# A decoder layer on one core: projection columns reordered, differential heads made two jobs, output projection begun at the sparse heads' rows, late modulation moved to VectorE

## The chip, the cores and the metric

The kernel runs on one core of one Trainium2 chip. The metric is the device time of one execution in microseconds (us). The engines are TensorE (PE in the profile; PEld is its loading of weights into the array), VectorE (DVE), ScalarE (ACT), GpSimd (POOL) and SyncE (SP), which here issues nearly all the transfers from HBM. Each engine works through its own queue in order; an instruction that waits holds up everything behind it on that engine.

## The reference

One layer of a transformer on 256 tokens of width 2048, all in float32, batch 1:

```python
mod = silu(c) @ w_ada + b_ada                          # 2048 x 12288, six chunks of 2048
shift_a, scale_a, gate_a, shift_f, scale_f, gate_f = split(mod, 6)
h = rms_norm(x, g_attn_pre) * (1 + scale_a) + shift_a
d_q, d_k, d_v, s_q, s_k, s_v, i_q, i_k, i_w = split(h @ w_in)      # 2048 x 5456
# partial rotary on d_q, d_k, s_q, s_k, i_q, i_k
diff_out = (softmax(q1 k1) - lam * softmax(q2 k2)) @ d_v           # 8 heads, causal
diff_out = rms_norm(diff_out, g_diff_sub) * (1 - lam_init)
score = sum over 16 heads of i_w * relu(i_q i_k)                   # the indexer
dsa_out = softmax(s_q s_k over the 64 best keys by score) @ s_v    # 8 heads, causal
mixed = concat(diff_out, dsa_out) @ w_o                            # 2048 x 2048
x = x + gate_a * rms_norm(mixed, g_attn_post)
h = rms_norm(x, g_ffn_pre) * (1 + scale_f) + shift_f
ff = (silu(h @ w_gate) * (h @ w_up)) @ w_down                      # d_ff = 5632
out = x + gate_f * rms_norm(ff, g_ffn_post)
```

## The kernel before, in words

**Weight products.** The 256 tokens are two tiles of 128 (t = 0, 1); the rows of a weight matrix are K tiles of 128. `wload` (line 148) brings a block of weights, one megabyte as a rule (4 K tiles x 512 columns), into one of RAW = 5 buffers `raw`, and splits it exactly into two parts: ScalarE copies the high part `whi` (line 168), VectorE subtracts it to get the low part `wlo` (line 169), each over 1024 columns at a time, into WB = 3 buffers each. `mm3` (line 176) makes three products for every K tile and token tile: high by high, high by low, low by high (lines 178, 181, 182).

**Modulation.** `ada_block` (line 191) queues the products of silu(c) with columns of w_ada in units of one megabyte. A unit is either made on TensorE (line 225; the K tiles go to four column groups of the array side by side) or on VectorE (line 233: acc = w * c + acc, 512 columns at a time). One call of `ada_step` uses one unit, and loads run AHEAD = 2 units ahead. `ada_cols` makes shift and scale as columns, for `modA` (attention) and `modF` (feed-forward), `ada_gate` makes the gates `Ga` and `Gf` as rows. Of each gate and of `modF` there are four blocks of 512 columns. On VectorE are two blocks of `Ga` (GA_DVE), one of `modF` (F_DVE) and all of `Gf`; the rest is on TensorE. A block's sums are turned to columns by small products at lines 282 (made on TensorE) or 286 (made on VectorE).

**Input projection.** The rows are taken in five groups of 1, 1, 2, 4 and 8 K tiles (GROUPS), each over all 5456 columns, since the modulation of a group must be known before its products; partial sums are collected in `PR` (line 733). The last group goes column block by column block, 512 wide (the last, number 10, is 336 wide), in the order (0, 2, 4, 10, 9, 8, 1, 3, 5, 6, 7); each column block is two megabyte blocks. 0 to 5 are the queries, keys and values of the differential heads, 6 and 7 the queries of the sparse heads, 8 to 10 the shared key and value, the indexer and its weights. After each column block `attend` rotates the columns and puts jobs in a list: `diff_head` (five stages s0 to s4, one job for each of 8 heads), `idx_pairs`, `top_k`, `dsa_pair` (four stages, one job for each pair of sparse heads). `attn_step` moves every job in flight by one stage and admits the next one of the list; it is called once after each megabyte block. `ada_step` is called there too, with RATE (1, 1, 1, 2) units.

**Output projection.** Row block a = 0, 4, 8, 12 of w_o (rows 0 to 7 of its 16 K tiles are the differential heads', 8 to 15 the sparse heads'), for column blocks 0 and 1 together; before each, `need_mix` runs stages until the heads of these rows are written to `mixT`. Column blocks 2 and 3 follow in `tail_pair`, which ends token tile 0 before token tile 1, so that the norm (`residual`, line 836) and the transposed, modulated input `H2` of the feed-forward (`h2_tiles`, line 826) begin early. After each block there is one `ada_step` and one `attn_step`.

**Feed-forward.** The second half of `H2` (K tiles 8 to 15) needs the second half of `modF`. So the first NSPLIT = 2 column blocks of w_gate and w_up are first multiplied over K tiles 0 to 7 alone (line 875, the half phase), the sums parked in `part` (line 887) and completed later (line 909); meanwhile up to FRATE = 2 modulation units follow each block.

**Order of instructions.** The program text gives the dependences and the priority; the order on each engine is laid out by a planner with estimated times, which takes the earliest instruction in the text that is ready. Only instructions marked `keep_in_program_order` keep their place.

## Time and profile before

| | us |
|---|---|
| median of 3 runs | 1275.33 |
| lowest and highest run | 1273.48, 1276.99 |
| profiled execution: span from first to last instruction | 1272.5 |
| TensorE busy | 1233.9 |
| VectorE busy | 774.3 |
| ScalarE busy | 560.9 |
| GpSimd busy | 21.4 |

The profiled execution's time is recorded as its span alone. A busy time counts an instruction from its start to its end; the ends of matmuls are modelled and products overlap their successors, so the distance between the starts of two products says more about TensorE than their durations. A float32 product (modulation, transposes, attention) appears as two instructions; weight products appear as one each. The stages stand at: input projection's last group until about 395 us, output projection 395 to 511.5, feed-forward from about 516.

### The profile page before, as it was taken

How to read it: one execution, taken by the hardware profiler on the slowest of the kernel's cores; microseconds unless marked ns; L12 is line 12 of the kernel's file. 1: busy time of each engine (PE TensorE's matmuls, PEld its weight loads, DVE VectorE, ACT ScalarE, POOL GpSimd, SP SyncE). 2: the span in 40 equal slices, each digit the busy share in tenths (PEclk: the TensorE clock that was granted, in tenths of full speed). 3: DMA queues.
4: the chain of work that ended last, by engine and by line, in shares of the span. 5: the costliest groups of instructions: out<-in, count | busy, mean ns of one | idle time of the engine just before them, and what ended most of it. 6: DMA issues, size and time to landing. Idle time of an engine off the chain costs nothing.

```text
span 1272.5 us, 15272 instructions
## 1 busy us (share of the span) xinstructions
PE 1233.9 (97%) x5938; PEld 950.3 (75%) x5938; DVE 774.3 (61%) x1160; ACT 560.9 (44%) x806; POOL 21.4 (2%) x55
## 2 busy tenths in 40 slices
PE   4999999999999999899999999999999999999996
PEld 3666666777666786688887888888888888888885
DVE  3576455898598683758867545754455454445565
ACT  4733333345345543764444444444444334444442
POOL 1000000000000000200000000000000000000000
PEclk8999999999999999999999999999999999999998
DMA  9999997978687487858878656766556555565541
GB/s 307 339 343 327 347 381 278 314 263 321 211 285 268 142 329 289 306 167 286 282 264 290 200 193 222 251 227 198 176 189 199 190 188 190 194 198 182 184 164 66
DMA packets 160090, 310.13 MB, mean 244 GB/s; under 512 B 5785, under 2 KB 19978, under 8 KB 158738
## 3 DMA queue, kind: packets, MB, share of 16 engines
q1 hardware_dynamic: 159938, 309.14, 70.7%
q8 instruction: 46, 0.75, 0.2%
q14 instruction: 26, 0.21, 0.0%
q10 hardware_dynamic: 80, 0.02, 0.0%
HBM read 307.05 MB, written 2.10 MB: 243 GB/s over the span
## 4 chain that ended last, share of the span: by engine, by line
PE 88%; DMA 4%; DVE 4%; issue 1%; ACT 1%; SPq 1%; POOL 0%; DVEq 0%; POOLq 0%; ACTq 0%
PE mm L181 26%; PE mm L178 26%; PE mm L182 25%; PE ad L225 5%; DMA raw<-in_w_ada_dram 4%; DVE aacc L233 2%; DVE wlo L169 1%; PE tr L474 1%; PE tr L411 1%; PE tr L918 1%; PE tr L830 1%; SPq L211 1%; PE tr L392 1%; PE tr L301 0%; PE tr L282 0%
## 5 line engine op out<-in xcount | busy, mean ns | idle before, releaser
L169 DVE TENSOR_TENSOR wlo<-raw,whi 128x1024 fp32r<-128x1024 f32 (+1 forms) x383 | 462.3, 1212 | 338.6 <-ACT whi L168 337.7
L168 ACT ACTIVATE whi<-raw 128x1024 fp32r<-128x1024 f32 (+1 forms) x383 | 400.3, 1050 | 522.4 <-PE mm L182 458.1
L181 PE MATMUL mm<-wlo,h 128*128 128x512 f32 (+1 forms) x1056 | 416.8, 395 | 1.9 <-DVE wlo L169 1.9
L182 PE MATMUL mm<-whi,h 128*128 128x512 f32 (+1 forms) x1056 | 409.9, 389 | 0.2 <-DVE h L335 0.2
L178 PE MATMUL mm<-whi,h 128*128 128x512 f32 (+1 forms) x1056 | 381.4, 394 | 2.4 <-ACT h L330 1.4
L181 PEld LDWEIGHTS mm<-wlo,h 128*128 128x128 f32 x1056 | 198.9, 188 | 62.5 <-issue 9.5
L178 PEld LDWEIGHTS mm<-whi,h 128*128 128x128 f32 x1056 | 196.8, 188 | 63.2 <-issue 13.6
L182 PEld LDWEIGHTS mm<-whi,h 128*128 128x128 f32 x1056 | 198.3, 188 | 42.5 <-issue 3.0
L181 PE MATMUL mm<-wlo,gT 128*128 128x512 f32 x348 | 135.8, 390 | 0.0
L182 PE MATMUL mm<-whi,gT 128*128 128x512 f32 x348 | 135.4, 389 | 0.0
L178 PE MATMUL mm<-whi,gT 128*128 128x512 f32 x348 | 123.0, 390 | 0.0
L233 DVE SCALAR_TENSOR_TENSOR aacc<-raw,csil,aacc 128x512 f32<-128x512 f32 x126 | 94.1, 746 | 23.8 <-DMA raw<-in_w_ada_dram 22.5
L225 PE MATMUL ad<-raw,c 128*32 128x512 f32 (+2 forms) x640 | 79.6, 537 | 9.9 <-DMA raw<-in_w_ada_dram 9.9
L733 DVE TENSOR_TENSOR PR<-mm,PR 128x512 f32<-128x512 f32 (+1 forms) x88 | 57.1, 669 | 41.2 <-PE mm L182 41.0
L182 PEld LDWEIGHTS mm<-whi,gT 128*128 128x128 f32 x348 | 65.3, 188 | 13.8 <-issue 0.2
L181 PEld LDWEIGHTS mm<-wlo,gT 128*128 128x128 f32 x348 | 65.3, 188 | 13.7 <-issue 0.2
L178 PEld LDWEIGHTS mm<-whi,gT 128*128 128x128 f32 x348 | 65.3, 188 | 13.4
L181 PE MATMUL mm<-wlo,mixT 128*128 128x512 f32 x124 | 49.1, 397 | 0.0
L178 PE MATMUL mm<-whi,mixT 128*128 128x512 f32 x124 | 47.5, 400 | 0.6 <-ACT mixT L587 0.6
L182 PE MATMUL mm<-whi,mixT 128*128 128x512 f32 x124 | 46.4, 399 | 0.0
L225 PEld LDWEIGHTS ad<-raw,c 128*32 128x32 f32 x640 | 17.6, 116 | 36.4 <-issue 31.3
L181 PEld LDWEIGHTS mm<-wlo,mixT 128*128 128x128 f32 x124 | 23.3, 188 | 7.8 <-issue 2.5
(195 smaller groups left out, 678.8 us busy)
## 6 DMA issues: line engine op xcount, KB each, us to landing
raw<-in_w_ada_dram SPq DMA_DIRECT2D x96, 1024.0 KB, 7.1
raw<-in_w_gate_dram SPq DMA_DIRECT2D x44, 1024.0 KB, 5.2
raw<-in_w_up_dram SPq DMA_DIRECT2D x44, 1024.0 KB, 5.1
raw<-in_w_down_dram SPq DMA_DIRECT2D x44, 1024.0 KB, 5.2
raw<-in_w_in_dram SPq DMA_DIRECT2D x39, 1024.0 KB, 6.9
raw<-in_w_o_dram SPq DMA_DIRECT2D x16, 1024.0 KB, 5.0
xx<-in_x_dram SPq DMA_DIRECT2D x2, 1024.0 KB
x<-in_x_dram SPq DMA_DIRECT2D x2, 1024.0 KB, 4.7
```

The source lines that it names most:

```text
L168: ACT.activation(hv, src, AF.Copy)
L169: DVE.tensor_tensor(lv, src, hv.bitcast(F32), op=ALU.subtract)
L178: i = PE.matmul(ps, lhsT=hi, rhs=whi, start=start, stop=False)
L181: PE.matmul(ps, lhsT=hi, rhs=wlo, start=False, stop=False)
L182: PE.matmul(ps, lhsT=lo, rhs=whi, start=False, stop=stop)
L211: SP.dma_start(st[b, u], ada_w[u * kk * P:(u + 1) * kk * P, col0s[b]:col0s[b] + n] .rearrange("(k p) n -> p k n", p=P))
L225: PE.matmul(st["ps"][32 * j:32 * j + 32, :n], lhsT=c33[:, k, 1 - b:33 - b], rhs=w, start=(b == 0 and k < 4), stop=(b == nb - 1 and k >= 12 ...
L233: DVE.scalar_tensor_tensor(acc, w, csil[:, k:k + 1], acc, op0=ALU.mult, op1=ALU.add)
L392: PE.transpose(tr[:, i * P:(i + 1) * P], PR[:, t, c0:c0 + P], ident)
L411: PE.matmul(sc[i][:, SEG[t]], lhsT=st["q"][r, (2 * j + t) * P:(2 * j + t + 1) * P], rhs=ikT[r, :P * (t + 1)], start=True, stop=True)
L474: PE.matmul(sc[i][:, SEG[t]], lhsT=l, rhs=r, start=False, stop=(t == T - 1))
L733: DVE.tensor_tensor(dst, banks[c0][t][:, :n], dst, op=ALU.add)
```

## The change

- The last group's column order becomes (10, 9, 8, 0, 2, 4, 6, 7, 1, 3, 5).
- `diff_head` makes two jobs: queries and keys to the probabilities (s0 to s2), put in the list after the key columns, and values to `mixT` (s3, s4), put there after the value columns. The probabilities wait in a buffer for five heads. A job has a set of conditions, and `attn_step` admits the first job of the list whose conditions are met; `top_k` waits for all indexer heads, `dsa_pair` for the selection.
- In the last group `attn_step` is called inside the block, after every second K tile: twice per megabyte block, where it was once.
- The output projection takes its first two column blocks in row order 8, 12, 0, 4.
- The second 1024 columns of `modF` are made on VectorE as one block of 1024 columns (before: 512 of them on VectorE, 512 on TensorE). The VectorE halves of `Ga` and all of `Gf` are blocks of 1024 columns too, so an accumulation is 1024 wide.
- RATE becomes (1,), FRATE 1, NSPLIT 4: the half phase covers four column blocks instead of two.
- Buffers are shared: the selection mask takes the indexer keys' place, the rotation's two scratch tiles take that of the heads' outputs, the last split of `tail_pair` that of the second parking buffer. The tile `c33` is made a little later in the text.

The diff, cut to its core:

```diff
-GA_DVE = (2, 3)
-F_DVE = (2,)
-RATE = (1, 1, 1, 2)
-ATT = 1
-FRATE = 2
+RATE = (1,)
+FRATE = 1
-NSPLIT = 2
+NSPLIT = 4
...
-                    hi = more.tile([P, 1024], F32R, tag="xhi", name=nm("xhi"))
-                    lo = more.tile([P, 1024], F32R, tag="xlo", name=nm("xlo"))
+                    both = more.tile([P, 2, 1024], F32R, tag="part", name=nm("xhl"))
+                    hi, lo = both[:, 0], both[:, 1]
...
-            st["acc", b] = wp.tile([P, 512], F32, tag="aacc", name=nm("aacc"), bufs=2)
+            st["acc", b] = wp.tile([P, 1024], F32, tag="aacc", name=nm("aacc"), bufs=2)
...
-    def ada_gate(G, chunk, col, on_pe):
+    def ada_gate(G, chunk, col, n, on_pe=False):
...
-            ps = tr_bank()
-            PE.matmul(ps, lhsT=ones, rhs=accs[0], start=True, stop=True)
-            DVE.tensor_tensor(G[:, col:col + 512], ps, G[:, col:col + 512], op=ALU.mult)
+            for a in range(0, n, 512):
+                ps = tr_bank()
+                PE.matmul(ps, lhsT=ones, rhs=accs[0][:, a:a + 512], start=True, stop=True)
+                g = G[:, col + a:col + a + 512]
+                DVE.tensor_tensor(g, ps, g, op=ALU.mult)
...
-        m1 = pp.tile([P, P], F32, tag="rp1", name=nm("rp1"), bufs=1)
-        m2 = pp.tile([P, P], F32, tag="rp2", name=nm("rp2"), bufs=1)
+        m = pp.tile([P, 2, P], F32, tag="on", name=nm("rp"), bufs=2)
+        m1, m2 = m[:, 0], m[:, 1]
...
-    def attn_step(admit=1):
-        for _ in range(admit):
-            if jobs:
-                active.append(jobs.pop(0))
+    def attn_step():
+        ready = next((j for j in jobs if done.issuperset(j[0])), None)
+        if ready is not None:
+            jobs.remove(ready)
+            active.append(list(ready[1]))
...
-        return [head] + [lambda r=r: rounds(r) for r in range(0, TOPK // 8, 2)] + [tail]
+        return {("idx", i) for i in range(8)}, [head] + [lambda r=r: rounds(r) for r in range(0, TOPK // 8, 2)] + [tail]
...
-            st["a"] = p_T(s[:, 0])
+            p_T(s[:, 0], heads["a"][:, h % 5])
+            done.add(("a", h))
...
-        return [s0, s1, s2, s3, s4]
+        free = {("v", h - 5)} if h >= 5 else set()
+        return (free, [s0, s1, s2]), ({("a", h)}, [s3, s4])
...
-            newjobs.extend([diff_head(4 * (ci - 2) + j) for j in range(4)])
+            for j in range(4):
+                h = 4 * (ci - 2) + j
+                qk, heads[h] = diff_head(h)
+                newjobs.append(qk)
+        elif ci in (4, 5):
+            newjobs.extend([heads[4 * (ci - 4) + j] for j in range(4)])
...
-    order = (0, 2, 4, 10, 9, 8, 1, 3, 5, 6, 7)
+    order = (10, 9, 8, 0, 2, 4, 6, 7, 1, 3, 5)
...
-    for b in range(4):
-        ada_gate(Ga, 2, b * 512, b not in GA_DVE)
+    ada_gate(Ga, 2, 0, 512, True)
+    ada_gate(Ga, 2, 512, 512, True)
+    ada_gate(Ga, 2, 1024, 1024)
     need_ga = len(units)
-    for b in range(4):
-        ada_cols(modF, 3, bF, gF, b * 512, 512, b not in F_DVE)
-        if b == 1:
-            need_f1 = len(units)
+    for b in range(2):
+        ada_cols(modF, 3, bF, gF, b * 512, 512, True)
+    need_f1 = len(units)
+    ada_cols(modF, 3, bF, gF, 1024, 1024, False)
     need_f2 = len(units)
...
+                    if last and k % 2 == 0:
+                        attn_step()
...
                 ada_step(RATE[bi % len(RATE)])
-                for _ in range(ATT):
-                    attn_step()
...
-    for a in (0, 4, 8, 12):
+    for a in (8, 12, 0, 4):
...
-                    mm3(banks[ci, t], mt, k, t, whi, wlo, k == 0, k == KT - 1)
+                    mm3(banks[ci, t], mt, k, t, whi, wlo, k == 8, k == 7)
...
-            for b in range(4):
-                ada_gate(Gf, 5, b * 512, False)
+            for b in range(2):
+                ada_gate(Gf, 5, b * 1024, 1024)
```

## Rows read from the trace of the kernel before

**Rows 1.** The page's first part: busy us, share of the span and instructions of each engine.

```profile
PE 1233.9 (97%) x5938; PEld 950.3 (75%) x5938; DVE 774.3 (61%) x1160; ACT 560.9 (44%) x806; POOL 21.4 (2%) x55
```

**Rows 2.** The order of time on TensorE in the feed-forward: start us, modelled duration us, engine, line, operation.

```profile
799.78 0.39 PE L178 MATMUL mm<-whi,h 128*128 128x512 f32 x1
800.01 0.39 PE L181 MATMUL mm<-wlo,h 128*128 128x512 f32 x1
800.24 0.39 PE L182 MATMUL mm<-whi,h 128*128 128x512 f32 x1
```

**Rows 3.** The table by stretches: stretch in us, its length, then busy us (and instructions) of PE, PEld, DVE, ACT, POOL, granted TensorE clock, DMA share, GB/s.

```profile
235.00:300.00 65.00, 65.00 (x339) 48.51 (x333) 59.80 (x144) 30.84 (x71) 3.54 (x4) 1.00 0.87 305
300.00:395.00 95.00, 95.00 (x502) 61.90 (x502) 68.28 (x189) 41.63 (x82) 1.38 (x2) 1.00 0.74 259
395.00:426.00 31.00, 26.00 (x147) 19.59 (x144) 25.64 (x66) 15.80 (x53) 3.17 (x3) 1.00 0.68 238
...
511.50:523.00 11.50, 7.80 (x56) 3.77 (x56) 8.50 (x15) 7.11 (x17) 5.41 (x9) 1.00 0.82 294
523.00:600.00 77.00, 77.00 (x371) 63.67 (x370) 53.75 (x89) 47.48 (x80) 1.21 (x3) 1.00 0.71 246
...
800.00:840.00 40.00, 40.00 (x178) 33.14 (x177) 23.36 (x24) 17.01 (x17) 0.00 (x0) 1.00 0.84 289
```

**Rows 4.** The chain that ended last, in order of time, around the end of the output projection: start us, us, what (line and number of instructions).

```profile
494.47 0.34 PE tr L286 x4
494.81 0.97 PE ad L225 x2
496.21 0.98 PE ad L225 x2
498.77 1.00 PE ad L225 x8
501.13 0.98 PE ad L225 x4
502.54 0.98 PE ad L225 x2
...
527.64 1.00 PE ad L225 x8
532.95 0.79 PE tr L282 x8
```

**Rows 5.** The order of time on TensorE at the norm between output projection and feed-forward; in brackets the idle time before an instruction and what ended it.

```profile
511.64 2.78 PE L225 MATMUL ad<-raw,c 128*32 128x512 f32 x24
516.57 2.05 PE L830 MATMUL tr<-dg,x 128*128 128x128 f32 x16 [2.15 <-POOL dg L848]
...
519.03 1.06 PE L225 MATMUL ad<-raw,c 128*32 128x512 f32 x8
```

**Rows 6.** The same view at the start of the output projection, three of its waits.

```profile
411.01 0.44 PE L586 MATMUL tr<-ident,on 128*128 128x128 f32 x2 [0.69 <-ACT qT L395]
412.01 0.50 PE L178 MATMUL mm<-whi,mixT 128*128 128x512 f32 x1 [0.56 <-ACT mixT L587]
...
416.87 1.07 PE L495 MATMUL tr<-ident,s 128*128 128x128 f32 x6 [1.13 <-DVE s L519]
```

**Rows 7.** Groups of instructions by line and shape, whole span: line, engine, operation, count, busy us, mean ns of one, idle time of the engine before them and what ended it.

```profile
L169 DVE TENSOR_TENSOR wlo<-raw,whi 128x1024 fp32r<-128x1024 f32 x374 | 455.4, 1223 | 334.9 <-ACT whi L168 334.0
...
L233 DVE SCALAR_TENSOR_TENSOR aacc<-raw,csil,aacc 128x512 f32<-128x512 f32 x126 | 94.1, 746 | 23.8 <-DMA raw<-in_w_ada_dram 22.5
...
L843 DVE SCALAR_TENSOR_TENSOR x<-y,ry,x 128x1024 f32<-128x1024 f32 x4 | 5.0, 1281 | 1.8 <-POOL ry L145 1.8
```

**Rows 8.** The table by stretches again, for DMA (last two columns: share of the 16 engines, GB/s): one row of the whole table, and one of the table for line 233 alone (busy us and count of that line, clock, DMA share, GB/s).

```profile
40.00:80.00 40.00, 38.40 (x207) 26.01 (x210) 32.27 (x54) 22.68 (x37) 0.00 (x0) 1.00 1.00 353
...
460.00:470.00 10.00, 3.85 (x6) 1.00 1.04 385
```

**Rows 9.** Groups by line and shape on VectorE from 235 to 396 us, columns as in rows 7.

```profile
L169 DVE TENSOR_TENSOR wlo<-raw,whi 128x1024 fp32r<-128x1024 f32 x35 | 42.5, 1219 | 13.8 <-ACT whi L168 13.6
L233 DVE SCALAR_TENSOR_TENSOR aacc<-raw,csil,aacc 128x512 f32<-128x512 f32 x29 | 21.6, 744 | 0.1
L733 DVE TENSOR_TENSOR PR<-mm,PR 128x512 f32<-128x512 f32 x16 | 10.7, 682 | 0.1
```

**Rows 10.** The same on TensorE from 235 to 396 us.

```profile
L181 PE MATMUL mm<-wlo,h 128*128 128x512 f32 x120 | 48.9, 407 | 0.0
...
L225 PE MATMUL ad<-raw,c 128*32 128x512 f32 x134 | 18.3, 602 | 0.0
...
L181 PE MATMUL mm<-wlo,mixT 128*128 128x512 f32 x16 | 6.3, 397 | 0.0
...
L182 PE MATMUL mm<-whi,h 128*128 128x336 f32 x16 | 5.1, 318 | 0.0
```

**Rows 11.** The table by stretches (columns as in rows 3) behind the last product and early in the span; the clock is the third column from the end.

```profile
1262.20:1265.60 3.40, 0.00 (x0) 0.00 (x0) 2.55 (x5) 0.72 (x2) 0.00 (x0) 1.00 0.69 255
1265.60:1272.50 6.90, 0.00 (x0) 0.00 (x0) 2.91 (x6) 0.00 (x0) 0.55 (x1) 0.50 0.40 152
...
23.20:33.30 10.10, 7.58 (x69) 4.96 (x69) 0.75 (x3) 1.50 (x4) 0.00 (x0) 0.50 1.10 351
```

More of the change, by code (lines that the diff above doesn't have):

```diff
@@ L206, in load @@
                 if not on_pe:
-                    POOL.memset(st["acc", b], 0.0)
-                SP.dma_start(st["acc", b][0:1], brow)
+                    POOL.memset(st["acc", b][:, :n], 0.0)
+                SP.dma_start(st["acc", b][0:1, :n], brow)
             raw = wp.tile([P, 2048], F32, tag="raw", name=nm("raw"), bufs=RAW)
@@ L293, in ada_cols @@
         ada_block([chunk * D + col, (chunk + 1) * D + col], n, on_pe, finish)
-    def ada_gate(G, chunk, col, on_pe):
+    def ada_gate(G, chunk, col, n, on_pe=False):
         c0 = chunk * D + col
         def finish(accs):
-            ps = tr_bank()
-            PE.matmul(ps, lhsT=ones, rhs=accs[0], start=True, stop=True)
-            DVE.tensor_tensor(G[:, col:col + 512], ps, G[:, col:col + 512], op=ALU.mult)
-        ada_block([c0], 512, on_pe, finish, b_ada[0:1, c0:c0 + 512])
+            for a in range(0, n, 512):
[3 more added lines that the diff above has]
+                DVE.tensor_tensor(g, ps, g, op=ALU.mult)
+        ada_block([c0], n, on_pe, finish, b_ada[0:1, c0:c0 + n])
+    ph1 = ExitStack()
+    pp = ph1.enter_context(tc.tile_pool(name="pp", bufs=1))
+    c33 = ct([P, KT, 33], "c33")
+    POOL.memset(c33, 0.0)
+    DVE.tensor_copy(c33[:, :, 1], csil)
     ssx = ct([P, T], "ssx")
@@ L369, in layer @@
     score = pp.tile([P, 384], F32, tag="score", name="score")
-    nsel = pp.tile([P, 384], F32, tag="nsel", name="nsel")
-    nselb = pp.tile([P, 384], BF16, tag="nselb", name="nselb")
+    nselb = []
     iwS = pp.tile([P, T, 16], F32, tag="iwS", name="iwS")
@@ L424, in pair @@
                 acc_started[0] = True
-        return [s0, lambda: pair(0), lambda: pair(1)]
+            done.add(("idx", p0 + j))
+        return set(), [s0, lambda: pair(0), lambda: pair(1)]
     jobs, newjobs, active = [], [], []
-    def attn_step(admit=1):
-        for _ in range(admit):
-            if jobs:
-                active.append(jobs.pop(0))
+    done = set()
+    def attn_step():
[3 more added lines that the diff above has]
+            active.append(list(ready[1]))
         for j in list(active):
@@ L441, in top_k @@
         m8 = pp.tile([P, T, 8], F32, tag="m8", name="m8")
+        nsel = pp.tile([P, 384], F32, tag="nsel", name="nsel")
         def head():
@@ L458, in tail @@
             DVE.tensor_tensor(nsel, nsel, score, op=ALU.is_equal)
-            DVE.tensor_scalar(nselb, nsel, NEG, None, op0=ALU.mult)
-        return [head] + [lambda r=r: rounds(r) for r in range(0, TOPK // 8, 2)] + [tail]
+            nselb.append(pp.tile([P, 384], BF16, tag="ikT", name="nselb"))
+            DVE.tensor_scalar(nselb[0], nsel, NEG, None, op0=ALU.mult)
+            done.add("sel")
+        return {("idx", i) for i in range(8)}, [head] + [lambda r=r: rounds(r) for r in range(0, TOPK // 8, 2)] + [tail]
     mixT = [None]
@@ L489, in softmax_parts, with p_T @@
         return s, l
-    def p_T(s2d):
+    def p_T(s2d, o=None):
         tr = tr_bank()
@@ L495, in p_T @@
             PE.transpose(tr[:, i * P:(i + 1) * P], s2d[:, i * P:(i + 1) * P], ident)
-        o = pp.tile([P, 384], F32, tag="pT", name=nm("pT"), bufs=2)
+        if o is None:
+            o = pp.tile([P, 384], F32, tag="pT", name=nm("pT"), bufs=2)
         ACT.activation(o, tr[:, :384], AF.Copy)
@@ L536, in s3 @@
             mixed.update((k, k + 1))
-        return [s0, s1, s2, s3]
+        return {"sel"}, [s0, s1, s2, s3]
+    heads = {}
     def diff_head(h):
@@ L543, in diff_head @@
         st = {}
+        if not heads:
+            heads["a"] = pp.tile([P, 5, 384], F32, tag="h1", name="aT")
         def s0():
@@ L555, in s2 @@
             s, l = st["s"], st["l"]
-            rl = st["rl"] = pp.tile([P, 2, T], F32, tag="rcp", name=nm("rcp"), bufs=4)
+            rl = st["rl"] = pp.tile([P, 2, T], F32, tag="rcp", name=nm("rcp"), bufs=6)
             DVE.reciprocal(rl, l)
@@ L562, in s2 @@
                                          s[:, 0, SEG[t]], op0=ALU.mult, op1=ALU.add)
-            st["a"] = p_T(s[:, 0])
+            p_T(s[:, 0], heads["a"][:, h % 5])
+            done.add(("a", h))
         def s3():
-            aT, rl = st["a"], st["rl"]
+            done.add(("v", h))
+            aT, rl = heads["a"][:, h % 5], st["rl"]
             v0, v1 = PR[:, 0, cv:cv + P], PR[:, 1, cv:cv + P]
@@ L790, in side @@
         ada_step(1)
-        for _ in range(ATT):
-            attn_step()
+        attn_step()
     def need_mix(ks):
```

7 lines of the change are left out of this document (1 added, 6 removed).

## The prediction

> **What bounds the kernel now.** Read the page's busy table first: TensorE is busy 97% of the span, VectorE 61% [rows 1]. Busy is not peak, so look next at a stretch of the feed-forward: successive weight products start 0.227 us apart [rows 2], and TensorE has no idle time there [rows 3]. A block (one megabyte of weights: 4 K tiles, 2 token tiles, 3 products) is 24 x 0.2275 = 5.46 us of TensorE. So time is won only by taking instructions off TensorE's queue or by closing its idle time. The table by stages shows where idle time is left: 5.0 us at 395 to 426 (start of the output projection) and 3.7 us at 511.5 to 523 (the norm between output projection and feed-forward, "the seam" below); 235 to 395 has none [rows 3]. The change can reach these two places and the modulation products; I find no edit that reaches the first 235 us (the same instructions in the same order) or the feed-forward behind its half phase.
>
> The profiled span is 1272.5 us, the median of the runs 1275.3; the profiled execution's own time is not recorded, so I put the 2.8 us between them around the span and add the sum to 1275.3.
>
> **The change part by part.**
>
> *1. The last quarter of the feed-forward modulation leaves TensorE.* It is 2 x 16 products of 512 columns; each is two instructions, four products run side by side, and eight instructions take 1.0 us. The records show 58 of its 64 instructions. In the chain of waits six pieces from 494.8 to 527.6 carry them: 0.97 + 0.98 + 1.00 + 0.98 + 0.98 + 1.00 = 5.91 us [rows 4]. The other 24 at 511.64 and 8 at 519.03 stand where TensorE waits for the norm anyway (the next item, the transposes at 516.57, still waited 2.15 us) [rows 5]: taking those away is worth nothing. Bringing the sums to columns changes too: a VectorE block needs 16 one-column products per 1024 columns, so 32 instructions where 16 and 8 stood: 16 more at 0.34 / 4 = 0.085 us are 1.4 us, less the 0.79 us piece at 532.95 [rows 4], +0.6. Together **-5.3 us**, bounds -4.5 and -6.5 (each run of these products also delays the next weight product by some 0.1 us).
>
> *2. Output projection from the sparse heads' rows on.* In the old order the sparse heads come last: when the projection's columns end, two differential heads and all four sparse pairs are unfinished, and TensorE has only rows 0 to 3 of the output weights to work on. Its queue then stands behind attention: 0.69 us for a copied transpose, 0.56 for mixT, 1.13 for the softmax rows [rows 6], 5.0 us in all [rows 3]. In the new order, counting stages as written, all four sparse pairs end a column and a half before the projection does, and four blocks on rows 8 to 15 and two on rows 0 to 3, 6 x 5.46 = 32.8 us, are ready while the last stages of heads 4 to 7 run in the first five of them. I take the whole idle time: **-5.0 us**. Bounds: 0, if the same chains stand in the queue a column earlier, and -6.4 (about nine waits each also lose the 0.16 us by which a product overlaps the next).
>
> *3. Seam.* Chain: VectorE's gating, two additions to the residual of 1.28 us each [rows 7], squares on ScalarE, GpSimd, transposes. The new VectorE modulation may stand before one of its steps: one 1024-wide accumulation, 1.28 us by the nearest row of that form and width [rows 7]. Bounds 0 and two of them, 2.6; I take half of one, **+0.6**.
>
> *4. VectorE and DMA in the longer half phase.* 1024-wide accumulations: 128 x 0.746 = 95.5 us of VectorE become 80 x 1.281 = 102.5 [rows 7]; 7 us more over 1.2 ms on an engine with a third free. What matters is density. Written steps: 22 in the last group and 14 in the output projection leave 12 of the 48 megabytes needed for the second half of h2; the half phase has 16 blocks and does one after each. Such a block costs VectorE 2 x 1.223 + 2 x 1.281 = 5.0 of 5.46 us, and 2.1 MB of DMA in 5.46 us is 384 GB/s. The trace shows 385 GB/s over one stretch of 10 us and 353 over another of 40 us [rows 8]. At 353 the 12 blocks (25.2 MB) need 71.3 us against 65.5: +5.8. Five raw buffers and three split ones run ahead, and four blocks without modulation follow: **+1.0**, bounds 0 and 5.8. The second half of h2 must then be ready when the half phase ends, 4 x 5.46 = 21.8 us later; it hides there. The eight more parked banks cost one copy and one addition each, 0.68 us by the addition of a bank [rows 9], on ScalarE and VectorE, which are busy 47 and 54 of 77 us at 523 to 600 [rows 3].
>
> *5. Denser attention in the projection.* Stages now advance twice per block. Columns 2, 4, 6, 7 (8 blocks) hold on VectorE 16 splits (19.5 us), 8 x 2 accumulations (20.5), 8 additions of a bank (5.5) and top-k with most of the heads. Attention and rotation on VectorE in the whole stage is what is left of 59.8 + 68.3 us after 42.5, 21.6 and 10.7: 53 us, some 50 without narrower forms [rows 3, 9]; a half to two thirds, 25 to 33, falls here: 70 to 79 us. TensorE there has 43.7 us of weights and, by the same shares of its own rest (160 - 3 x 136 x 0.2275 - 48 x 0.155 - 17 = 43 us, by the counts in [rows 10], 17 us being 134 modulation instructions at eight per 1.0; 0.155 us is about 0.2275 scaled to the 336-wide column), 21 to 29 us: 65 to 73. VectorE lags by about 6, up to 14 us where the shares differ; three split buffers are 3 x 2.73 = 8.2 us ahead. In 235 to 300 VectorE was busy 92% and TensorE never idle [rows 3]. So **+1.0**, bounds 0 and 14.
>
> The remaining edits (shared buffers, a prepared constant made later in the text, removed comments) cost nothing: the buffers are handed on only after their readers, which lie earlier in the same queues. If a rotation did wait for a head's buffer, the same lag as in 5 would grow.
>
> Sum: -5.3 - 5.0 + 0.6 + 1.0 + 1.0 = -7.7; 1275.3 - 7.7 = **1267.6 us**.
>
> **Rivals.**
>
> *A. VectorE sets the pace in columns 2 to 7* (the slower side). Top-k is a chain on VectorE alone, so it fills that engine without leaving gaps for the splits, and every weight product waits for its split. Price: the whole lag of 14 instead of 1: 1267.6 + 13 = 1281. It decides from a loss of about 11.5 us, where the gains are spent and 0.3% more. For it: VectorE is denser here than anywhere in the old trace. Against: 235 to 300, where denser work met no idle TensorE [rows 3].
>
> *B. The seam lets the clock fall.* Without the 24 products TensorE idles from 511.6 to 516.6, 4.9 us in one piece. At the end of the span the granted clock was still 1.00 for the 3.4 us after the last product and 0.50 from then on; early on it stood at 0.50 for 10.1 us after sparse work [rows 11]. Half of 10.1 is 5.0: up to 1273. The Trainium skill, TensorE: Matmul & The Clock Gate, section What's actually happening, says the throttled level is the default and activity releases it; by that this edit takes away what kept the clock up, which no row of the seam can show yet.
>
> *C. DMA limits the half phase*: +5.8 instead of +1.0, 1272.4. The Trainium skill, DMA: Bandwidth & Descriptors, section Specifications, gives about 358 GB/s per core from HBM and speaks against this part: an estimate by it is 25.2 / 358 = 70.4 us, +4.9. The trace's 40 us stretch (353) agrees, its 10 us stretch (385) does not.
>
> *D. The reorder does not do what it says*: the waits of part 2 reappear in front of the last column. Only part 1 pays: 1272.6.
>
> *E. Better*: part 2 at -6.4, no costs of 3 to 5: 1263.6, and 1262 with part 1 at its bound.
>
> **How the numbers follow.** Chances: forecast 0.47 (own range 1264 to 1271.4), A 0.18, B 0.09, C 0.07, D 0.06, E 0.13. A run of this kernel can be told from no change at about 0.3%, 3.8 us: faster is below 1271.5, slower above 1279.2. Faster: 0.47 + 0.13 = 0.60. Same: B, C, D, 0.22. Slower: A, 0.18. The range goes from E's better bound to just past A's price: 1261 to 1282.
>
> **What would show it.** Part 1: 64 fewer modulation instructions on TensorE (576), none between 494 and 530. Part 2: idle TensorE at the start of the output projection under 1.5 us. Part 3: the seam's idle time rises to about 5 us on the first wait, at clock 1.00 (0.50 is B). Part 4: the half phase, now twice as long, without idle TensorE; idle with splits waiting for raw is C. Part 5: the last group without idle; weight products waiting for VectorE's splits is A. I am wrong if idle time appears in the projection, or if the stages' TensorE sums fall by less than 5 us.

## The result and the profile after

The changed kernel takes 1290.8 us (median of 4 runs, 1287.8 to 1292.6) where the kernel before took 1274.4 beside it: ratio 1.0123, 95% interval 1.0103 to 1.0143. It is slower by 16.4 us; the forecast was faster by 7.7, and the measured time lies above the whole forecast range, 1261 to 1282. The profiled span is 1287.2 us (before 1272.5). One run of one variant below (new order, values first), 1907.7 us at a mean granted clock of 0.64, is slow and left out of its numbers.

The busy table of the page, changed kernel [rows 1]: TensorE has 64 modulation instructions fewer (line 219, 576 in all) and yet a longer span.

```profile
PE 1228.2 (95%) x5882; PEld 956.8 (74%) x5882; DVE 788.4 (61%) x1118; ACT 564.9 (44%) x813; POOL 20.2 (2%) x52
```

The table by stretches, changed kernel, columns as in [rows 3]:

```profile
235.00:300.00 65.00, 65.00 (x312) 46.66 (x311) 61.56 (x117) 27.02 (x42) 0.95 (x1) 1.00 0.81 294
300.00:350.00 50.00, 50.00 (x260) 36.43 (x259) 36.25 (x93) 23.68 (x50) 0.70 (x1) 1.00 0.77 268
350.00:400.00 50.00, 41.26 (x240) 26.28 (x239) 28.20 (x90) 20.28 (x57) 2.11 (x3) 0.93 0.65 222
400.00:430.00 30.00, 27.74 (x158) 20.70 (x157) 13.63 (x34) 14.23 (x37) 0.00 (x0) 1.00 0.54 192
430.00:480.00 50.00, 40.15 (x173) 30.27 (x172) 30.87 (x63) 20.37 (x59) 3.65 (x4) 0.80 0.50 175
...
500.00:540.00 40.00, 30.86 (x136) 25.34 (x135) 32.37 (x44) 20.62 (x41) 6.36 (x10) 0.87 0.74 262
540.00:620.00 80.00, 80.00 (x379) 66.77 (x378) 52.24 (x62) 41.39 (x59) 1.85 (x2) 1.00 0.73 250
```

Subtract the second number of a row from the first. In the projection, 235 to 350, TensorE has no idle time, although VectorE is busy 61.56 of the first 65 us. Behind it TensorE idles 8.7, 2.3, 9.9 and 9.1 us in the stretches that begin at 350, 400, 430 and 500, together 30.0. The same four stretches before had 0, 5.0, 0.0 and 3.7, together 8.7. The 21.3 us of new idle time, less the 4.5 to 6.5 us by which the modulation was to shorten the same stretch, are 15 to 17, and the spans differ by 14.7: the loss is idle TensorE between 350 and 540 us. The granted clock fell with it: in the kernel before it was 1.00 from 235 to 540, here it was 0.50 (1.2 instead of 2.4 GHz) in four stretches of 350 to 480, 27.3 us together, the longest behind the wait at 441.5:

```profile
441.90:455.60 13.70, 11.45 (x44) 8.75 (x43) 6.62 (x21) 4.57 (x19) 1.38 (x2) 0.50 0.01 1
```

What ends the idle time, from TensorE's order of time in the changed kernel (brackets: idle time before, and what ended it):

```profile
351.25 2.78 PE L219 MATMUL ad<-raw,c 128*32 128x512 f32 x24
...
359.46 1.48 PE L219 MATMUL ad<-raw,c 128*32 128x512 f32 x8 [3.39 <-DMA raw<-in_w_ada_dram]
...
365.61 0.33 PE L601 MATMUL tr<-ident,on 128*128 128x128 f32 x1 [2.77 <-DVE on L595]
...
374.52 0.76 PE L502 MATMUL tr<-ident,s 128*128 128x128 f32 x4 [2.24 <-DVE s L527]
...
404.86 1.06 PE L219 MATMUL ad<-raw,c 128*32 128x512 f32 x8 [2.17 <-DMA raw<-in_w_ada_dram]
...
441.52 0.30 PE L502 MATMUL tr<-ident,s 128*128 128x128 f32 x1 [3.31 <-DVE s L574]
...
463.14 0.50 PE L172 MATMUL mm<-whi,mixT 128*128 128x512 f32 x1 [1.46 <-ACT mixT L602]
...
520.06 0.39 PE L176 MATMUL mm<-xhl,mixT 128*128 128x512 f32 x1
...
527.04 3.76 PE L851 MATMUL tr<-dg,x 128*128 128x128 f32 x16 [6.59 <-POOL dg L869]
...
534.32 0.80 PE L172 MATMUL mm<-whi,h 128*128 128x512 f32 x1 [2.01 <-DMA raw<-in_w_gate_dram]
```

Three kinds of waits make up the 30.0 us. About 15 are the waits of [rows 6], more of them: steps of one head's or pair's chain between TensorE, VectorE and ScalarE, with no weight product to put between. The two waits at L219, 3.39 and 2.17 us, are for weights of the modulation: TensorE had taken three units in a row at 351.25, and the load that it then waited for was issued only at 352.38, when a buffer came free.

```profile
352.38 0.37 SPq L205 DMA_DIRECT2D raw<-in_w_ada_dram  x1
```

The last 9.1 us are the seam's, 2.01 of them for the first weights of `w_gate`. When the values reach `mixT` is told by the instructions on VectorE that write it (count, ns of one, first and last start): heads 0 to 3, then the four sparse pairs.

```profile
L603 DVE SCALAR_TENSOR_TENSOR mixT<-tr,g,mixT x4: 477/478/481, 351.0 to 367.7; 128x256 fp32r<-128x256 f32 x4
L542 DVE TENSOR_TENSOR mixT<-tr,mixT x4: 683/684/684, 380.2 to 414.6; 128x512 fp32r<-128x512 f32 x4
```

The projection's last product starts at 350.9 us (before 375.5, not the "about 395" that the text ahead of the change gives for the stage). So the sparse rows, with which the output projection begins, are written 29 to 64 us after TensorE has run out of projection. Milestones on TensorE's order of time (the 97th product is the first behind four blocks of 24) put the loss where it arose:

| start of | before | after | difference | forecast up to here |
|---|---|---|---|---|
| last product of the projection | 375.5 | 350.9 | -24.6 | |
| last product of the output projection | 511.3 | 520.1 | +8.8 | -9.3 (parts 1, 2, 5) |
| 97th recorded product of the feed-forward | 549.9 | 561.1 | +11.2 | -8.7 (part 3) |
| first product on `gT` | 708.9 | 722.1 | +13.2 | -7.7 (part 4) |
| last product on `gT` | 1261.8 | 1276.7 | +14.9 | -7.7 |

The last column adds up whole parts. By place, part 1's pieces at 527.64 and 532.95 (1.00 and 0.79 us) lie behind the output projection and its one-column products (32 at 0.085 us, 2.7) behind the 97th product, so that the forecast was -10.3, -11.5 and -7.7 at the second to the fourth mark.

### The profile page after: what moved, and what is told of

Its sections match the earlier page's. It is cut to its first block, busy times and chain, and to the rows that moved or that the text cites. A ratio compares the mean times of both kernels' runs of the same rounds, so it can differ in the third digit from the quotient of the medians.

```text
span 1287.2 us, 15112 instructions
## 1 busy us (share of the span) xinstructions
PE 1228.2 (95%) x5882; PEld 956.8 (74%) x5882; DVE 788.4 (61%) x1118; ACT 564.9 (44%) x813; POOL 20.2 (2%) x52
## 4 chain that ended last, share of the span: by engine, by line
PE 89%; DVE 3%; DMA 3%; ACT 1%; issue 1%; SPq 1%; POOL 0%; DVEq 0%; POOLq 0%; ACTq 0%
PE mm L175 27%; PE mm L172 27%; PE mm L176 26%; PE ad L219 4%; DMA raw<-in_w_ada_dram 3%; DVE wlo L163 1%; PE tr L481 1%; PE tr L939 1%; PE tr L410 1%; DMA raw<-in_w_gate_dram 1%; SPq L205 1%; PE tr L851 0%; PE tr L391 0%; ACT s L494 0%; PE tr L502 0%
## 5 line engine op out<-in xcount | busy, mean ns | idle before, releaser
L175 PEld LDWEIGHTS mm<-wlo,h 128*128 128x128 f32 x1056 | 198.9, 188 | 62.5 <-issue 10.2
L172 PEld LDWEIGHTS mm<-whi,h 128*128 128x128 f32 x1056 | 197.5, 188 | 59.0 <-issue 12.2
L227 DVE SCALAR_TENSOR_TENSOR aacc<-raw,csil,aacc 128x1024 f32<-128x1024 f32 x78 | 100.1, 1284 | 25.0 <-DMA raw<-in_w_ada_dram 22.6
L219 PE MATMUL ad<-raw,c 128*32 128x512 f32 (+2 forms) x576 | 65.9, 530 | 16.4 <-DMA raw<-in_w_ada_dram 16.4
L219 PEld LDWEIGHTS ad<-raw,c 128*32 128x32 f32 x576 | 14.6, 114 | 37.3 <-issue 25.8
L172 PEld LDWEIGHTS mm<-whi,mixT 128*128 128x128 f32 x124 | 24.4, 197 | 10.7 <-ACT mixT L602 2.5
```

Source lines behind the costliest of these rows:

```text
L172: i = PE.matmul(ps, lhsT=hi, rhs=whi, start=start, stop=False)
L175: PE.matmul(ps, lhsT=hi, rhs=wlo, start=False, stop=False)
L219: PE.matmul(st["ps"][32 * j:32 * j + 32, :n], lhsT=c33[:, k, 1 - b:33 - b], rhs=w, start=(b == 0 and k < 4), stop=(b == nb - 1 and k >= 12 ...
L227: DVE.scalar_tensor_tensor(acc, w, csil[:, k:k + 1], acc, op0=ALU.mult, op1=ALU.add)
```

## The experiments

All edits are to the changed kernel; "..." marks what is left out of a diff. "One step" is one attention step behind each block, as before; "old order" is the old column and row order. Ratios are to the kernel before, measured beside each (1273.6 to 1274.7 us).

**One half each.** The first kernel undoes the modulation (RATE, FRATE, NSPLIT and the blocks of `Ga`, `modF` and `Gf` as before), the second undoes attention (order, whole heads without conditions, one step behind each block):

```diff
-    order = (10, 9, 8, 0, 2, 4, 6, 7, 1, 3, 5)
+    order = (0, 2, 4, 10, 9, 8, 1, 3, 5, 6, 7)
...
-        return (free, [s0, s1, s2]), ({("a", h)}, [s3, s4])
+        return set(), [s0, s1, s2, s3, s4]
...
-                    if last and k % 2 == 0:
-                        attn_step()
...
+                attn_step()
...
-    for a in (8, 12, 0, 4):
+    for a in (0, 4, 8, 12):
```

> The changed kernel with its modulation part undone: blocks of 512 columns, the last quarter of the feed-forward modulation on TensorE, RATE (1, 1, 1, 2), FRATE 2, NSPLIT 2; columns, jobs and output rows stay new. Theory (order): the sparse heads are written only 30 us after the projection's last product, so TensorE runs dry at the start of the output projection and again before the last heads' rows whatever the modulation does; the seam returns to about 4 us of idle time: 1282 to 1286. Rival (modulation): VectorE and the seam are the whole loss: 1270 to 1275.

Measured: 1301.6 us, 1.0217 (1.0202 to 1.0232). Both expectations missed: beside the new attention the modulation part saves 11 us.

> The changed kernel with its attention part undone: old column order, one job for each differential head, one attention step per block, output rows 0, 4, 8, 12; the modulation part stays new (late half on VectorE, 1024 wide, NSPLIT 4). Theory (order): the idle time at 351 to 380 and 437 to 470 is gone; left are the 5 us less of modulation products and the longer seam at a lower clock: 1272 to 1278. Rival (modulation): 1286 to 1292.

Measured: 1272.6 us, 0.9985 (0.9976 to 0.9995). The whole loss is in attention's edits: this kernel's output projection ends at 503.4 us, the changed kernel's 16.6 later, and behind that mark the two take the same time to 0.6 us. The table by stretches of this kernel:

```profile
350.00:400.00 50.00, 48.72 (x265) 28.85 (x264) 37.27 (x121) 20.39 (x53) 1.38 (x2) 1.00 0.75 253
400.00:430.00 30.00, 27.77 (x163) 19.59 (x162) 16.45 (x49) 17.18 (x50) 1.38 (x2) 1.00 0.54 178
430.00:480.00 50.00, 49.95 (x257) 42.09 (x256) 38.87 (x57) 25.43 (x47) 0.00 (x0) 1.00 0.79 292
...
500.00:540.00 40.00, 30.98 (x141) 25.58 (x141) 31.74 (x51) 22.90 (x47) 6.37 (x10) 0.87 0.68 235
```

The idle time at 350 (1.3 us left of 8.7) and 430 is gone, that of the seam (500 to 540) is as in the changed kernel.

**The order, alone and undone.** First the rows alone (those of heads 0 to 3 in front), then both orders undone with the two jobs and the denser steps kept:

```diff
-    for a in (8, 12, 0, 4):
+    for a in (0, 8, 12, 4):
```

> The changed kernel with one line other: output rows in the order 0, 8, 12, 4. Theory (order): the rows of heads 0 to 3 are ready 12 to 29 us before the first sparse rows, so two blocks of products (11 us) fill the gap behind the projection, but they are missing later, in front of the last heads: 1282 to 1288. If idle time only moves to the second gap: 1289 to 1292. Rival (modulation): as the changed kernel, 1289 to 1292.

Measured: 1288.3 us, 1.0106 (1.0091 to 1.0121); not told apart from the changed kernel.

> The changed kernel with the column order (0, 2, 4, 10, 9, 8, 1, 3, 5, 6, 7) and the row order 0, 4, 8, 12 of the kernel before; two jobs for each differential head, two attention steps per block and the modulation part stay new. Theory (order): 1272 to 1279, as with the whole attention part undone, since the order alone decides which rows are ready. If the density of steps or the two jobs are the cause: 1283 to 1291.

Measured: 1291.4 us, 1.0135 (1.0117 to 1.0154). My theory that the order is the cause fell.

**Density, two jobs, order: one at a time.** Next come one step in the changed kernel; the two jobs alone, with old order and one step; the order alone, with whole heads and one step.

> The changed kernel with one attention step after each block, as before; new column and row order, two jobs for each head, new modulation. Theory: the denser steps are the cause, because they put stages into TensorE's and VectorE's queues between the halves of a block, and the projection runs on past them: 1272 to 1278 us, and the projection's last product at about 364 instead of 351 us. Rival one, the two jobs (the values' half is admitted late): 1286 to 1293, as the changed kernel. Rival two, half and half: 1279 to 1285.

> Old column order, old row order, one attention step after each block, new modulation; only the two jobs for each head with their conditions are new in attention. Theory (density): 1271 to 1276 us, as with all of attention undone (1272.6). Rival (two jobs): 1286 to 1293, as the kernel with old order and denser steps (1291.4).

> New column order and new row order, but heads in one job and one attention step after each block; new modulation. If the order costs nothing by itself, as the kernel with only the order undone suggests: 1269 to 1276 us. Rival: the order costs by itself, and that kernel hid it because the denser steps had already cost the same time: 1280 to 1290.

Measured: 1291.1 us, 1.0127 (1.0106 to 1.0147); 1311.2 us, 1.0289 (1.0271 to 1.0306); 1277.4 us, 1.0015 (1.0001 to 1.0029). The theory of denser steps fell: without them the changed kernel is as slow, and the two jobs alone cost 38.6 us, more than either side expected. The order alone lies between its two expectations, nearer the first. `attn_step` admits one job a step, and there are eight jobs more.

**A values' job admitted beside another job**, old order and one step, then new order and one step; and the denser steps with whole heads (old order; the heads listed after the value columns):

```diff
-        ready = next((j for j in jobs if done.issuperset(j[0])), None)
-        if ready is not None:
...
+        for vals in (True, False):
+            ready = next((j for j in jobs if done.issuperset(j[0])
+                          and any(c[0] == "a" for c in j[0]) == vals), None)
+            if ready is not None:
...
```

> Old column and row order, one attention step after each block, two jobs for each head as in the kernel that took 1311.2 us; but a step now admits a values' job beside another job, so that 12 values' jobs and other jobs no longer share one admission a step. Counted as written, every stage then stands within two blocks of where it stands with whole heads (1272.6 us). Theory (the two jobs cost by taking admissions: one a step, 8 more jobs, 8 blocks of 5.46 us at most): 1271 to 1277 us. Rival (the two jobs cost by their buffers or by their conditions): 1295 to 1311.

> New column and row order, two jobs, one attention step after each block, and a values' job admitted beside another job. Theory (admissions): within 3 us of the kernel with the order alone, 1275 to 1281, and 10 to 16 us better than the changed kernel, where the steps are twice as dense. Rival (the two jobs cost in some other way): 1288 to 1293, as with one admission a step (1291.1).

> Old column and row order, whole heads put in the list after the value columns, and the attention step after every second K tile, twice a block. If dense steps cost by themselves, since each holds fewer independent stages and the chain of one head stands closer together in the queues: 1285 to 1295, near the kernel with two jobs and dense steps (1291.4). Rival (dense steps cost nothing, and only the two jobs did): 1270 to 1278.

Measured: 1282.7 us, 1.0062 (1.0046 to 1.0078); 1285.5 us, 1.0086 (1.0067 to 1.0105); 1280.2 us, 1.0060 (1.0044 to 1.0075). All between the expectations: admission explains 28.6 of the 38.6 us, 10 are left, and denser steps cost something too (7.6 us, in a kernel that also lists the heads later). Where the 10 begin is seen on TensorE. With whole heads (attention undone) the first head's value products (line 584) start at 264.06, ahead of the next head's transposes (line 502):

```profile
264.06 0.39 PE L584 MATMUL tr<-PR,aT 128*128 128x128 f32 x2
...
270.44 0.27 PE L502 MATMUL tr<-ident,s 128*128 128x128 f32 x1
```

With two jobs and values admitted beside others the two change places (lines 586 and 504 there), and the value products come 12 us later:

```profile
269.52 0.27 PE L504 MATMUL tr<-ident,s 128*128 128x128 f32 x1
...
276.18 0.38 PE L586 MATMUL tr<-PR,aT 128*128 128x128 f32 x2
```

A step moves jobs in the order of admission. A whole head is the oldest when it comes to its values; a values' job is new, and stands behind younger heads that wait for VectorE.

**Values first inside a step**, in the same old-order kernel, in the changed kernel, and in the new order with one step (the diff is to the lines just added):

```diff
-                active.append(list(ready[1]))
+                job = list(ready[1])
+                if vals:
+                    active.insert(sum(j[-1] in last_v for j in active), job)
+                    last_v.append(job[-1])
+                else:
+                    active.append(job)
```

> As the kernel with old order, one step a block and values' jobs admitted beside others (1282.7 us), but inside a step the values' halves of heads come first and the queries' halves of younger heads behind them, as with whole heads. Theory (the order inside the step is what the two jobs still cost): 1271 to 1276 us, and the first head's value products at 264 to 266 us instead of 277. Rival (the conditions, by which the top-k selection and the sparse pairs stand a block later, cost the 10 us): 1280 to 1284.

Measured: 1275.1 us, 1.0001 (0.9991 to 1.0012), and the value products (line 591) are back in front:

```profile
263.83 0.39 PE L591 MATMUL tr<-PR,aT 128*128 128x128 f32 x2
...
270.20 0.27 PE L509 MATMUL tr<-ident,s 128*128 128x128 f32 x1
```

> The changed kernel (1290.8 us) with values' jobs admitted beside others and first inside a step; new order, two steps a block. Theory (order inside the step, with the denser steps a smaller cost of their own): 1279 to 1286. Rival (in the changed kernel the denser steps alone cost as much): 1288 to 1292.

Measured: 1287.8 us, 1.0101 (1.0080 to 1.0122): between the two, at the rival's edge.

> New column and row order, one step a block, two jobs with values' jobs admitted beside others (1285.5 us), and now first inside a step. Theory (order inside the step): 1275 to 1280, as with whole heads in the new order (1277.4). Rival: 1283 to 1287.

Measured: 1279.5 us, 1.0035 (1.0021 to 1.0049), as the theory said.

**The seam**, each on the kernel with attention undone (1272.6 us). 26 products of the output projection's input by itself, whose sums nobody reads, behind its last product (`fill`); no modulation step behind the last three blocks (QUIET = 3); GpSimd's small steps of the norm on VectorE:

```diff
+            for i in range(fill):
+                p = PE.matmul(f, lhsT=mt[:, 0, 0, :P], rhs=mt[:, 0, 0:2, :], start=i == 0,
+                              stop=i == fill - 1)
```

> All of attention undone, new modulation (1272.6 us as it was), and 26 extra products of 512 columns, whose sums nobody reads, behind the last weight product of the output projection: 26 x 0.227 = 5.9 us of the 6.6 us for which TensorE waits in the seam. Theory (the fallen clock is a cost of its own): the transposes there take 2.05 us instead of 3.78 and the first products of the feed-forward 0.23 apart instead of up to 0.6; 1269 to 1271 us. Rival (the slow products only fill time in which the next piece of the chain would be waited for anyway): 1271.5 to 1274.

Measured: 1273.7 us, 0.9995 (0.9985 to 1.0005). TensorE there:

```profile
511.38 2.05 PE L854 MATMUL tr<-dg,x 128*128 128x128 f32 x16 [0.71 <-POOL dg L872]
...
516.15 0.50 PE L176 MATMUL mm<-whi,h 128*128 128x512 f32 x1 [2.25 <-DVE h L337]
...
519.60 2.08 PE L854 MATMUL tr<-dg,x 128*128 128x128 f32 x8 [1.91 <-POOL dg L872]
```

The first transposes take 2.05 us for 16 instructions, as at full clock, and the next links of the chain are waited for instead. The fall was not prevented but put off: the granted clock was 0.50 from 518.8 to 525.6 (without the extra products from 508.6 to 515.4 and from 518.9 to 522.3), and the next eight instructions took 2.08.

```diff
-            side()
+            side((a, ci) not in blocks[-QUIET:])
...
-    def side():
-        ada_step(1)
+    def side(ada=True):
+        if ada:
+            ada_step(1)
```

> All of attention undone, new modulation (1272.6 us), and no modulation step after the last three blocks of the output projection, so that no 1024-wide accumulation stands on VectorE before the norm; the three units go to the longer half phase. Theory (the accumulations lengthen the chain of the norm by 1.3 to 2.6 us): the wait of 6.6 us in the seam falls to 4.5 to 5.5, 1270 to 1271.8 us. Rival (the chain is ScalarE's and GpSimd's, or the half phase pays the three units back): 1272 to 1274.

Measured: 1291.7 us, 1.0135 (1.0113 to 1.0158), a miss by 20 us: the wait grew to 8.57 us, and the second half of `H2` came too late (5.5 us idle at 620 to 700). Of the 15.0 us between the profiled spans 3.7 arise up to the 97th product and 11.1 between it and the first on `gT`.

```diff
-        POOL.tensor_tensor(sss[:, t:t + 1], ss1[:, t, 0:1], ss1[:, t, 1:2], op=ALU.add)
+        DVE.tensor_tensor(sss[:, t:t + 1], ss1[:, t, 0:1], ss1[:, t, 1:2], op=ALU.add)
```

(and the multiply-add and the scaling of `dg` behind it.)

> All of attention undone, new modulation (1272.6 us); in the norm of the seam GpSimd's addition of the two square sums, its multiply-add and the scaling of the diagonal move to VectorE, and only the power stays on GpSimd. Theory (these small steps are slow on GpSimd beside VectorE's splits, 1.6 and 1.3 us for what takes 0.2 and 0.6 when VectorE rests): the wait of 6.6 us in the seam falls by 1.5 to 2.5 and the time to 1269.5 to 1271.5. Rival (on VectorE they stand behind splits of 1.2 us each): 1272 to 1275.

Measured: 1278.9 us, 1.0030 (1.0021 to 1.0040), worse than the rival: the wait was 7.4 us. But the moved steps are not what cost most. In the profiled execution (1284.6 us) the output projection already ends 4.6 us later, 1.3 us arise up to the 97th product, and 5.8 between it and the first on `gT`, where products waited for the second half of `H2`.

**More products behind the norm.** Three and four blocks are multiplied first for token tile 0 and then for token tile 1, where it was two (`late` = 1, 2); splits wait in unwritten room of `H2`. The RATE shown is the second's; the first has one step more, `(1,) * 21 + (2,)`.

```diff
+        lates = [(nk - 8, ci) for ci in cs[2 - late:]]
-        blocks = [(a, ci) for a in range(0, nk - 4, 4) for ci in cs]
+        blocks = [(a, ci) for a in range(0, nk - 4, 4) for ci in cs if (a, ci) not in lates]
...
-RATE = (1,)
+RATE = (1,) * 20 + (2, 2)
```

> All of attention undone, new modulation (1272.6 us). At the end of the output projection three blocks instead of two are multiplied first for token tile 0 and then for token tile 1, one split half being kept in the room of the feed-forward input that is not written yet, so that token tile 1's products behind token tile 0's last are 36 instead of 24: 8.2 us instead of 5.5. The block takes no attention or modulation step; the projection makes up for it with one modulation step more. Theory (the seam's idle time is the norm's chain less these products): the wait falls from 6.6 to about 3.9 us, 1269 to 1271 us. Rival (the splits of the kept blocks stand in the norm's chain, or the two stretches only move): 1272 to 1276.

> The same with four blocks, 48 products for token tile 1, 10.9 us, three split halves kept in the feed-forward input's room, and two modulation steps more in the projection. Theory: the wait falls to 0 to 2 us, 1266 to 1269.5 us. Rival: 1272 to 1278.

Measured: 1284.1 us, 1.0076 (1.0062 to 1.0090), and 1285.0 us, 1.0084 (1.0070 to 1.0098). Misses in time. In the first the wait stayed (6.82 us), as the chain grew with its cover: this accumulation stood on VectorE in front of the norm, and had itself waited for its weights.

```profile
501.76 0.75 DVE L225 TENSOR_SCALAR aacc<-raw,csil 128x1024 f32<-128x1024 f32 x1 [3.16 <-DMA raw<-in_w_ada_dram]
```

In the second the seam did what was expected, no wait and full clock at the transposes, but the output projection ended at 515.2 us instead of 503.4 (4.6 us idle at 430 to 480):

```profile
515.74 2.05 PE L858 MATMUL tr<-dg,x 128*128 128x128 f32 x16
```

The edit put two modulation steps more into the end of the projection, where attention's chains decide; that these steps are the reason was not tried. The marks separate what the times mix. Against the kernel with attention undone the first variant lost 4.8 us up to the end of the output projection, won 1.7 from there to the 97th product, and lost 6.3 more up to the first product on `gT`; the second lost 11.8, won 5.2 and lost 5.7. So the seam covered in the second was worth about 5 us, and both variants lost more elsewhere, the last part where products waited for the second half of `H2` (in the second variant):

```profile
637.03 0.50 PE L172 MATMUL mm<-whi,h 128*128 128x512 f32 x1 [2.09 <-ACT h L332]
```

The same wait of 2.1 us, and the same loss of some 6 us, stand in the profiles of the norm on VectorE and of the changed kernel with values first (1287.8).

## Why the prediction was wrong

**The step that failed is part 2**, and with it part 5. Part 2 took the order in which stages are written for the order in time: "all four sparse pairs end a column and a half before the projection does", 32.8 us of products ready. Written, the last sparse pair ends in the first block of the last column but one; on the chip it ends 64 us after the projection's last product. A block of weight products needs nothing from attention and took its 5.5 us, while a stage is a chain over three engines. TensorE did not wait at 235 to 350; it went on with the projection and finished it 24.6 us early. Of these 11.2 are there with attention undone too (364.3), so attention's edits moved it by 13.4. The lag was not lost there. It was stored, and paid behind 350 us when no independent product was left. Part 5 saw the lag (6 to 14 us on VectorE) but expected it as weight products waiting for splits, as did rival A; no such wait is there. Part 2 expected the 5.0 us of idle time at the start of the output projection to go; at 350 to 480 there are 20.9. Parts 1, 2 and 5 together should have brought the end of the output projection forward by 9.3 us; it came 8.8 later.

**Which edit costs the time** the runs show as a ladder, each step between two kernels that differ in one thing, the last in two (differences of the ratios, times 1274.5 us). In the old order with one step: whole heads 0.9985; two jobs with their conditions, admitted beside others and placed first, 1.0001 (+2 us, hardly told apart); placed last in a step 1.0062 (+8); one admission a step 1.0289 (+29). To the changed kernel: whole heads, old order 0.9985; new order 1.0015 (+4); two jobs, well placed, 1.0035 (+2.5, not told apart); denser steps 1.0101 (+8); one admission and the last place 1.0123 (+3, not told apart). So the two jobs are dear by how they are admitted and placed, not by being two. The shares do not add up in a fixed way. From the new order with two jobs, well placed (1.0035), another way leads to the changed kernel: placed last 1.0086 (+6.5); one admission 1.0127 (+5, where it was 29 in the old order); denser steps 1.0123 (nothing). Denser steps cost about 8 us where admission and place are cured (1279.5 to 1287.8) and nothing where they are not (1291.1 without them, 1290.8 with). Shown is that placement, admission and density together cost some 11 us, and the order and the split some 6. Nor is all of it stored lag: with the order alone the output projection ends 2.2 us later than with attention undone, and 3.2 more arise in the seam, where the wait is longer (6.59 us there):

```profile
514.40 3.78 PE L847 MATMUL tr<-dg,x 128*128 128x128 f32 x16 [8.34 <-POOL dg L865]
```

I costed the split of heads, its conditions and the way it is admitted at nothing.

How the place in the text comes to decide is shown for one place only: the first head's value products, 12 us later when written behind another head's transposes, and back with that order alone. That it acts through the three transposing banks, which attention and modulation share in the order of the text, fits and was not tried; why denser steps cost 8 us is open too (between the two profiles 10.2 us arise up to the end of the output projection, 2.5 are won back in the seam and 5.5 lost behind the 97th product).

**Part 1** was right in size. With attention undone the output projection ends at 503.4 instead of 511.3 us, 7.9 earlier, of which 1.5 are attention's idle time at 350 to 430 (3.5 instead of 5.0): 6.4 for the modulation; by place part 1 had 6.3 ahead of this mark. Why it is worth 11 us beside the new attention is open.

**Part 3** was mis-sized: +0.6, bound 2.6. By the 97th product the kernel with attention undone had lost 3.1 of its 7.9 us, the changed kernel 2.4, although part 1's pieces of 1.79 us left this stretch too: the seam cost 4 to 5 us. From token tile 0's last product to the first transposes the changed kernel takes 12.2 us (514.9 to 527.0) instead of 10.5: on VectorE two accumulations stood before the last gating, not half of one. Its bank was read by ScalarE from 515.05 on, so the gating began some 1.1 us late:

```profile
513.65 2.60 DVE L227 SCALAR_TENSOR_TENSOR aacc<-raw,csil,aacc 128x1024 f32<-128x1024 f32 x2
516.17 0.68 DVE L790 TENSOR_TENSOR y<-mm,Ga 128x512 f32<-128x512 f32 x1
```

GpSimd's four steps took 3.88 us instead of 3.69 (523.11 to 526.99; before 512.82 to 516.51). The wait was 6.59 us instead of "about 5". Rival B came true as a fact: the granted clock was 0.50 from 523.8 to 530.7, and the transposes took 3.76 us instead of 2.05 [rows 5]. Its price is not settled: with other products in the wait the first transposes ran at full clock, which won nothing (1273.7), but the clock then fell a little later.

**Part 4**: from the 97th product to `gT` it takes 2.0 us more, without idle TensorE (80.00 of 80 at 540 to 620), so rival C did not come. Part 1's one-column products, which now stand here, were alone to cost 2.7, and two other products left the stretch (below); part 4's own +1.0 cannot be told apart in it. Another 1.7 us arose in the rest of the feed-forward, of which the prediction said that no edit reaches it. One does: two products of `Gf`'s blocks, now 1024 wide, moved behind the first product on `gT`, eight instructions on `ones` instead of four, 1.4 us. With attention undone the rest takes 554.6 us as in the changed kernel, with the modulation undone 552.9 as before.

**The rivals.** D (the waits reappear in front of the last column) had the right kind of wait, but a column too early, and priced it at what part 2 had claimed, 5 us; nothing in it let the waits grow. The range's upper end, 1282, was there for another mechanism, A's.

With attention undone the kernel is 1.9 us faster than before (0.9985). No variant measured was better.

## What to carry to other kernels

Where a list of stages only sets priority, work that depends on nothing overtakes it, so count a stage's end by its chain in the trace and not by its place in the text, and ask what TensorE will have left when the independent work is gone. A job split in two changes what the admission rule and the order inside a step do to it; keep both as they were, or test them alone. An edit that covers a wait must be read stretch by stretch: the chain behind the wait may grow by what the cover puts in front of it, and stages ahead of it and behind it may lose what it won.

## What the hardware showed

The same addition of one column to another on GpSimd (two per norm, one for each token tile) took 1.60 us while VectorE subtracted splits and 0.19 when VectorE was idle (532.95 to 534.10), in the changed kernel (start, us):

```profile
522.29 2.36 DVE L163 TENSOR_TENSOR wlo<-raw,whi 128x1024 fp32r<-128x1024 f32 x2
...
523.11 1.60 POOL L867 TENSOR_TENSOR sss<-ss 128x1 f32<-128x1 f32 x1 [5.37 <-ACT y L866]
...
533.45 0.19 POOL L867 TENSOR_TENSOR sss<-ss 128x1 f32<-128x1 f32 x1 [5.93 <-ACT y L866]
```

and 3.54 us in the kernel without modulation steps behind the last three blocks, beside an accumulation and two splits:

```profile
507.12 1.28 DVE L228 SCALAR_TENSOR_TENSOR aacc<-raw,csil,aacc 128x1024 f32<-128x1024 f32 x1
508.32 2.35 DVE L164 TENSOR_TENSOR wlo<-raw,whi 128x1024 fp32r<-128x1024 f32 x2
...
507.18 3.54 POOL L865 TENSOR_TENSOR sss<-ss 128x1 f32<-128x1 f32 x1 [6.46 <-ACT y L864]
```

Both long additions ended 0.05 to 0.06 us behind VectorE's second split (524.71 behind 524.65, 510.72 behind 510.67).

The Trainium skill, SBUF — State Buffer, section SBUF: two separate sides, says that VectorE and GpSimd share a pair of ports, and that of an operation of VectorE with two operands in SBUF and a GpSimd operation that reads SBUF the one that starts first holds it to its end while the other is blocked. The three rows agree with it, except that GpSimd waited through two or three instructions of VectorE in a row, not one; that they are the reason was not tried by itself.
